# Seven block products for two of the short convolution's three input branches

## The chip, the cores and the metric

The kernel runs on one core of a Trainium2 chip. The metric is the device time of one execution in microseconds (us). A core has a matrix engine (TensorE, PE in the profile; its weight loads are PEld), a vector engine (VectorE, DVE), a scalar engine (ScalarE, ACT), GpSimd (POOL), SyncE (SP), which here only issues transfers, and 16 DMA engines. Matmuls write to PSUM, eight banks of 2 KB on each of 128 partitions; everything else lies in SBUF.

## The reference, cut to what matters

A sequence of 512 tokens of width 1024 passes through a first block (attention with low rank projections, a convolution, a gated feed-forward layer, a gated embedding) and a second block of two layers. The change lies in the second block's first layer:

```python
def short_conv_mixer(h, w_in, conv_w, w_out):
    b_gate, c_gate, u = jnp.split(h @ w_in, 3, axis=-1)      # h: 512 x 1024, w_in: 1024 x 3072
    v = c_gate * u
    vp = jnp.pad(v, ((0, 0), (CONV_WIDTH_2 - 1, 0), (0, 0)))
    conv = sum(conv_w[k] * vp[:, k:k + S] for k in range(CONV_WIDTH_2))
    return (b_gate * conv) @ w_out

h = rms_norm_2(x, norm_mix[0])
x = x + short_conv_mixer(h, a_w_in[0], a_conv_w[0], a_w_out[0])
x = x + squared_relu_mlp(rms_norm_2(x, norm_mlp[0]), mlp_w1[0], mlp_w2[0])
```

Everything is in 32-bit floats.

## The kernel before

Activations lie transposed: a tile holds 128 channels on the partitions and 512 tokens along the free dimension, so 1024 channels are eight tiles, x[0] to x[7]. A 32-bit product is made of three matmuls on rounded parts: each operand is split into a high part (`whi`, `xgh`) and a remainder (`wlo`, `xgl`), and high by high, high by remainder and remainder by high are added in PSUM (L305 to L307 in `mm`).

A weight tile comes from `unit` (L265): SP loads a raw 128 x 1024 tile, ScalarE rounds it to the high part (L280), VectorE subtracts for the remainder (L281). Raw, high and remainder have two buffers each in pool `wp`. `gemm` (L314) multiplies such a tile by the eight tiles of activations: 24 matmuls of 512 columns into one PSUM bank.

The short convolution (L964 to L986) first splits x times the norm's gain into `xg` (L967). Then it runs a loop over eight tiles of output channels c. Each turn makes three gemms: `pc`, `pu` and `pb` (c_gate, u and b_gate). VectorE multiplies pc by the squared row scale R4s (L976) and by pu into the padded tile `gpad` (L979), ScalarE makes the last tap (L981), VectorE adds the other two (L983), multiplies by pb (L985), and the result is split into `hid` (L986). The next loop (L988) makes eight gemms of `hid` with the out weights and adds to x. The PSUM phase in this stage is `ps2` (L859): six banks `mm`, two banks `t`.

The MLP (L995) uses another product, `fast_pair` (L357), for pairs of output tiles. Two output tiles by two halves of the tokens make a 2 x 2 block product, computed with seven block products and not eight. Its moving operands are the two halves of two neighbouring activation tiles (slots B11 to B22) and four sums of them (T1 to T4), formed by `pair_sums` (L323): two scalings on ScalarE into a buffer `yh`, four steps on VectorE into a buffer `yl` (L329 to L332), and a split into `xt`; it is called four times, and `yh` and `yl` have one buffer each. Its weights come from `pair_units` (L339): a raw tile `a` with two weight blocks; a raw tile `s`, loaded by SP and then added to by a second transfer on POOL's queue (L344); a block `z`; two sums of these on VectorE (L351, L353); and the splits of all. `us` and `ua` use the two buffers of `wp`, and `z`, `yh` and `yl` have one each.

Each block product is 12 matmuls of 128 x 256. They run in the order B11, T1, B21, T2, B22, T3, T4. B11, T2, T3 and T4 add up in one bank `y1`, T1 and B22 in a bank `mm`, and each bank is read between two products. `fast_pair` calls `fill` twice between B22 and T4 and twice after T4, and in the MLP a fill is one product of the second layer, 12 matmuls of 512 columns.

The code is written in program order, and a scheduler fixes each engine's own order when the kernel is compiled, earlier places in the program first where instructions are ready; engines run their order in sequence. Buffers are handed out as they come free. SP issues nearly all transfers in one queue. POOL's queue carries `gpad`'s small memset (L978), the additions of L344, and a few elementwise steps.

## Time and profile before

| | us |
|---|---|
| median of 3 runs | 1980.68 |
| lowest, highest | 1980.64, 1984.46 |
| the profiled execution | 1979.01 |
| its span | 1977.2 |
| TensorE busy in it | 1876.5 |
| VectorE busy in it | 1331.9 |
| ScalarE busy in it | 957.0 |

The page of the profile gives busy time by engine, the span in 40 slices, and the chain of work that ended last. The trace can be asked for more: busy time by stretch, instructions in order of time, groups of instructions by line and shape, one line or one tile with what waited for it. A matmul's row gives its start and a modelled duration; as matmuls are pipelined, the distance between two starts is what one costs in a row of them. The short convolution's loop runs from about 713 to 851 us, its out product to 896, the first MLP's paired products from 910 to 1210, the second MLP's from 1632.

### The profile page before, as it was taken

The numbers are of one execution on the slowest core, as the hardware profiler recorded it, in microseconds if no ns is written. First come the engines' busy times: TensorE is split into PE (matmuls) and PEld (weight loads), VectorE is DVE, ScalarE is ACT, GpSimd is POOL, SyncE is SP. The second block draws the span as 40 slices with busy tenths as digits, with TensorE's granted clock in tenths as the row PEclk, the third lists the DMA queues.
The fourth block names the chain that finished last, engine by engine and source line by source line (L and its number), as shares of the span: only waits on it lengthen the run. The fifth ranks groups of instructions, "written<-read, shape, count | busy, mean of one in ns | idle before, by whom it ended". The sixth has DMA issues, their size and how long they took to land.

```text
span 1977.2 us, 27638 instructions
## 1 busy us (share of the span) xinstructions
PE 1876.5 (95%) x10198; PEld 1592.5 (81%) x10198; DVE 1331.9 (67%) x2277; ACT 957.0 (48%) x1755; POOL 420.1 (21%) x397
## 2 busy tenths in 40 slices
PE   8778989999999999999999999989999979999996
PEld 6556788888888978888988988778888778889895
DVE  7979676335444874476666666769887977666664
ACT  6566654333233442254444444546666755444443
POOL 2786240000001420010000002335454420000001
PEclk9889999999999999999999999999999989999998
DMA  4121222223323223233455453254323134554542
GB/s 147 54 67 41 79 82 86 96 96 96 93 90 106 74 76 96 96 119 105 128 144 144 128 141 94 90 163 118 78 84 84 31 100 130 144 132 134 139 107 75
DMA packets 82742, 202.11 MB, mean 102 GB/s; under 512 B 9904, under 2 KB 18288, under 8 KB 82608
## 3 DMA queue, kind: packets, MB, share of 16 engines
q1 hardware_dynamic: 77744, 184.88, 30.7%
q0 software_dynamic: 4032, 14.68, 4.3%
q8 instruction: 80, 1.31, 0.3%
q10 hardware_dynamic: 832, 0.79, 0.1%
q14 instruction: 54, 0.44, 0.1%
HBM read 187.73 MB, written 2.10 MB: 96 GB/s over the span
## 4 chain that ended last, share of the span: by engine, by line
PE 75%; DVE 13%; ACT 4%; issue 3%; DMA 3%; POOL 2%; SPq 0%; DVEq 0%; POOLq 0%; ACTq 0%
PE mm L305 18%; PE mm L306 18%; PE mm L307 18%; PE y L370 3%; PE y L372 3%; PE y L371 3%; DVE cy L605 2%; DVE wlo L281 2%; PE mm L372 2%; PE mm L371 2%; PE mm L370 2%; PE o L530 1%; PE s L497 1%; DVE pw L503 1%; PE t L522 1%
## 5 line engine op out<-in xcount | busy, mean ns | idle before, releaser
L280 ACT CAST whi<-raw 128x512 fp32r<-128x512 f32 (+4 forms) x342 | 260.7, 770 | 469.9 <-PE mm L306 370.7
L281 DVE TENSOR_TENSOR wlo<-raw,whi 128x512 fp32r<-128x512 f32 (+4 forms) x318 | 303.4, 960 | 108.0 <-ACT whi L280 102.6
L306 PE MATMUL mm<-hidl,whi 128*128 128x512 f32 (+1 forms) x794 | 300.1, 379 | 0.1
L305 PE MATMUL mm<-hidh,whi 128*128 128x512 f32 (+1 forms) x794 | 295.1, 379 | 5.1 <-ACT hidh L286 5.0
L307 PE MATMUL mm<-hidh,wlo 128*128 128x512 f32 (+1 forms) x794 | 297.7, 378 | 2.2 <-DVE wlo L281 2.1
L306 PE MATMUL mm<-xgl,whi 128*128 128x512 f32 (+1 forms) x608 | 234.0, 386 | 2.8 <-DVE xgl L290 2.8
L307 PE MATMUL mm<-xgh,wlo 128*128 128x512 f32 (+1 forms) x608 | 233.8, 386 | 0.0
L305 PE MATMUL mm<-xgh,whi 128*128 128x512 f32 (+1 forms) x608 | 232.9, 386 | 0.6 <-ACT whi L280 0.6
L305 PEld LDWEIGHTS mm<-hidh,whi 128*128 128x128 f32 x794 | 148.6, 188 | 32.4 <-ACT hidh L286 5.7
L307 PEld LDWEIGHTS mm<-hidh,wlo 128*128 128x128 f32 x794 | 149.2, 188 | 30.9 <-DVE wlo L281 3.2
L306 PEld LDWEIGHTS mm<-hidl,whi 128*128 128x128 f32 x794 | 149.2, 188 | 27.4 <-DVE hidl L287 0.9
L344 POOL DMA_DIRECT2D raw<-mlp1f x28 | 24.6, 879 | 551.8 <-DVE wlo L281 236.3
L306 PEld LDWEIGHTS mm<-xgl,whi 128*128 128x128 f32 x608 | 115.4, 190 | 28.6 <-DVE xgl L290 4.0
L305 PEld LDWEIGHTS mm<-xgh,whi 128*128 128x128 f32 x608 | 115.2, 190 | 26.0 <-ACT whi L280 1.5
L307 PEld LDWEIGHTS mm<-xgh,wlo 128*128 128x128 f32 x608 | 115.5, 190 | 24.4
L287 DVE TENSOR_TENSOR wlo<-raw,whi 128x1024 fp32r<-128x1024 f32 x56 | 68.5, 1222 | 84.2 <-ACT whi L286 84.1
L421 POOL TENSOR_TENSOR ssq<-ssq,sq 128x512 f32<-128x512 f32 (+1 forms) x58 | 71.4, 1230 | 252.0 <-ACT sq L418 251.1
L505 ACT ACTIVATE pw<-pw,nm 128x512 f32<-128x512 f32 (+3 forms) x160 | 89.4, 560 | 57.7 <-DVE nm L503 55.4
L286 ACT CAST whi<-raw 128x1024 fp32r<-128x1024 f32 x56 | 58.7, 1050 | 97.1 <-DMA raw<-mlp1f 78.4
L1027 DVE TENSOR_TENSOR x<-mm,x 128x512 f32<-128x512 f32 x116 | 79.4, 686 | 37.1 <-PE mm L307 37.0
L603 POOL TENSOR_TENSOR cy<-cy,tap 128x512 f32<-128x512 f32 x60 | 92.0, 1533 | 29.6 <-ACT tap L602 26.0
L605 DVE SCALAR_TENSOR_TENSOR cy<-cp,cols,cy 128x512 f32<-128x512 f32 x60 | 73.3, 1221 | 2.0 <-ACT cy L616 1.4
(835 smaller groups left out, 4695.7 us busy)
## 6 DMA issues: line engine op xcount, KB each, us to landing
raw<-mlp SPq DMA_DIRECT2D x140, 256.0 KB, 2.8
raw<-mlp1f SPq DMA_DIRECT2D x56, 512.0 KB, 3.7
raw<-mlp1f POOLq DMA_DIRECT2D x28, 512.0 KB, 6.5
raw<-a_in SPq DMA_DIRECT2D x24, 512.0 KB, 3.5
raw<-w_gate SPq DMA_DIRECT2D x22, 512.0 KB, 3.5
raw<-w_up SPq DMA_DIRECT2D x22, 512.0 KB, 3.5
raw<-w_down SPq DMA_DIRECT2D x16, 512.0 KB, 3.5
zraw<-mlp1f SPq DMA_DIRECT2D x28, 256.0 KB, 3.7
```

What stands on the lines that cost most here:

```text
L280: S.copy(hi[:, a], raw[:, a])
L281: eng.tensor_tensor(lo[:, a], raw[:, a], hi[:, a], op=OP.subtract)
L305: P.matmul(acc, hi[:, s], h, start=first and k == 0, stop=False)
L306: P.matmul(acc, hi[:, s], l, start=False, stop=False)
L307: P.matmul(acc, lo[:, s], h, start=False, stop=last and k == n - 1)
L370: P.matmul(acc, hi[:, s], h, start=first and j == 0, stop=False, skip_group_check=True)
L371: P.matmul(acc, hi[:, s], l, start=False, stop=False, skip_group_check=True)
L372: P.matmul(acc, lo[:, s], h, start=False, stop=j == 3, skip_group_check=True)
L505: S.activation(t, t, AF.Exp, bias=nm[:, i:i + 1], scale=-1.0, accum_out=rs[:, i:i + 1])
L603: G.tensor_tensor(conv_y[c], conv_y[c], t, op=OP.add)
L605: V.scalar_tensor_tensor(conv_y[c], cp[c][:, k:k + T], w, conv_y[c], op0=OP.mult, op1=OP.add)
L1027: V.tensor_tensor(x[m], acc, x[m], op=OP.add)
```

## The change

For c = 0 the three gemms stay. From c = 1 on, `pc` and `pu` are made by `fast_pair`, with weights packed for `pair_units` on the host (`a_inf`), and `pb` in two halves of 12 matmuls each, whose weights are half units (128 x 512) of a new pool `sw` with two buffers; the two halves are the first two calls of `fill`, and the later calls do nothing. `pair_sums` is called four times when c is 1. `pu` comes out negated, which the step into `gpad` takes back; `pc` and `pu` are now tiles in SBUF. The PSUM phase `ps2m` (two banks `y1`, four `mm`, two `t`) begins ahead of this loop and no longer ahead of the MLP. The pools `sw` and `xta` are released after the loop. The packed tensor `a_in` keeps the tiles that are still read as before.

```diff
--- before.py
+++ after.py
@@ -176,7 +176,9 @@
     A["w_down2"] = _units(w[2048:])
     A["w_ple_proj"] = _units(I["w_ple_proj"][0])
     A["w_ple_gate"] = _units(I["w_ple_gate"][0])
-    A["a_in"] = _units(I["a_w_in_2"][0])
+    w = np.asarray(I["a_w_in_2"][0])
+    A["a_in"] = _units(np.concatenate([w[:, :1152], w[:, 2048:2176]], 1))
+    A["a_inf"] = _blocks(w[:, 1024:].reshape(D, 2, 8, 128).transpose(0, 2, 1, 3)[:, 1:].reshape(D, -1))
     A["a_out"] = _units(I["a_w_out_2"][0])
     for l in range(2):
         A[f"mlp1_{l}"] = _units(I["mlp_w1_2"][l])[:4]
@@ -967,16 +969,32 @@
         split(x[k], *xg[k], col("norm_mix0", k))
     R4 = row_tile(r4)
     R4s = row_tile(r4, square=True)
+    sw, tpl = pool("swa"), pool("xta")
+    psum_phase("ps2m", y1=2, mm=4, t=2)
     hid = []
     for c in range(KT):
-        pc = gemm(A["a_in"][8 + c], xg)
-        pu = gemm(A["a_in"][16 + c], xg)
-        pb = gemm(A["a_in"][c], xg)
-        t = tmp()
+        if c == 0:
+            pc, pu, pb = [gemm(A["a_in"][i], xg) for i in (8, 9, 0)]
+        else:
+            if c == 1:
+                xps = [slots(xg[k:k + 2], pair_sums(k, "norm_mix0", sw, tpl)) for k in range(0, KT, 2)]
+            us = pair_units(A["a_inf"][c - 1], sw)
+            pb = bank("mm")
+            fill = [0, 1]
+
+            def gate_half(i, pb=pb, c=c):
+                u = unit(A["a_in"][c][:, 512 * i:512 * i + 512], pl=sw, size=512, bufs=(2, 2))
+                mm(pb, u, xg[4 * i:4 * i + 4], first=i == 0, last=i == 1)
+
+            pc, pu = fast_pair(us, xps, md, lambda: fill and gate_half(fill.pop(0)))
+        t = tmp() if c == 0 else pc
         V.tensor_tensor(t, pc, R4s, op=OP.mult)
         gpad = md.tile([128, 2 + T], FT, name="gpad", bufs=2)
         G.memset(gpad[:, :2], 0.0)
-        V.tensor_tensor(gpad[:, 2:], pu, t, op=OP.mult)
+        if c == 0:
+            V.tensor_tensor(gpad[:, 2:], pu, t, op=OP.mult)
+        else:
+            V.scalar_tensor_tensor(gpad[:, 2:], pu, -1.0, t, op0=OP.mult, op1=OP.mult)
         y = tmp()
         S.activation(y, gpad[:, 2:], AF.Copy, scale=col("a_conv_w", 3 * c + 2))
         for k in range(2):
@@ -984,6 +1002,8 @@
                                    op0=OP.mult, op1=OP.add)
         V.tensor_tensor(y, pb, y, op=OP.mult)
         hid.append(split_in(md, "hid", y, bufs=9))
+    tpl.release()
+    sw.release()
     sx = SumSq(8, whole=True)
     for m in range(KT):
         acc = gemm(A["a_out"][m], hid)
@@ -1083,7 +1103,6 @@
     def shared_norm(c, ts):
         S.copy(R5[:, ts], rows(c, None, ts)[:, ts])
 
-    psum_phase("ps2m", y1=2, mm=4, t=2)
     mlp(0, md, xg, sx, 5, shared_norm, shared)
     md.release()
     tp[0].release()
```

## Rows read from the trace of the kernel before

**Rows 1.** Part 1 of the page: busy time, share of span, instructions.

```profile
PE 1876.5 (95%) x10198; PEld 1592.5 (81%) x10198; DVE 1331.9 (67%) x2277; ACT 957.0 (48%) x1755; POOL 420.1 (21%) x397
```

**Rows 2.** Part 4 of the page: the chain that ended last, by line.

```profile
PE mm L305 18%; PE mm L306 18%; PE mm L307 18%; PE y L370 3%; PE y L372 3%; PE y L371 3%; DVE cy L605 2%; DVE wlo L281 2%; PE mm L372 2%; PE mm L371 2%; PE mm L370 2%; PE o L530 1%; PE s L497 1%; DVE pw L503 1%; PE t L522 1%
```

**Rows 3.** Busy time by stretch; columns in the first line.

```profile
core 0: us, PE busy (x) PEld busy (x) DVE busy (x) ACT busy (x) POOL busy (x), PEclk, DMA share, GB/s
713.20:726.70 13.50, 13.05 (x52) 10.01 (x52) 8.58 (x15) 5.00 (x8) 1.02 (x1) 0.87 0.10 40
...
735.00:851.00 116.00, 116.00 (x501) 94.05 (x501) 56.47 (x67) 30.81 (x38) 0.60 (x6) 1.00 0.30 97
...
960.00:1200.00 240.00, 240.00 (x1496) 215.38 (x1495) 157.70 (x248) 109.65 (x190) 9.45 (x11) 1.00 0.51 135
1631.80:1652.00 20.20, 17.88 (x105) 15.07 (x105) 17.88 (x30) 12.72 (x23) 0.92 (x1) 1.00 0.56 147
```

**Rows 4.** Timeline, start of the short convolution: start, duration, engine.

```profile
721.53 0.75 DVE L290 SCALAR_TENSOR_TENSOR xgl<-x,cols,xgh 128x512 fp32r<-128x512 f32 x1
...
713.23 0.58 PE L306 MATMUL mm<-xgl,whi 128*128 128x512 f32 x1 [1.81 <-DVE xgl L290]
```

**Rows 5.** Timeline of TensorE, short convolution: first and last of 57 rows.

```profile
759.80 0.39 PE L306 MATMUL mm<-xgl,whi 128*128 128x512 f32 x1
...
772.82 0.39 PE L305 MATMUL mm<-xgh,whi 128*128 128x512 f32 x1
```

**Rows 6.** Timeline of TensorE, first MLP: rows 1 and 49 of 49.

```profile
1005.48 0.28 PE L370 MATMUL y<-xg0h,whi 128*128 128x256 f32 x1
...
1011.18 0.39 PE L305 MATMUL mm<-hidh,whi 128*128 128x512 f32 x1
```

**Rows 7.** View of line 985: durations min/median/max, first and last start.

```profile
L985 DVE TENSOR_TENSOR tmp<-mm,tmp x8: 681/692/692, 740.2 to 851.1; 128x512 f32<-128x512 f32 x8
```

**Rows 8.** View of tile xt0h: one weight load of the MLP.

```profile
L370 PEld LDWEIGHTS mm<-xt0h,whi x28: 187/189/192, 923.3 to 1911.3; 128*128 128x128 f32 x28
```

**Rows 9.** Groups by line and shape, 960 to 1200 us, VectorE: busy, mean ns.

```profile
L281 DVE TENSOR_TENSOR wlo<-raw,whi 128x512 fp32r<-128x512 f32 x46 | 31.0, 684 | 2.5 <-ACT whi L280 2.3
L287 DVE TENSOR_TENSOR wlo<-raw,whi 128x1024 fp32r<-128x1024 f32 x23 | 28.1, 1222 | 37.2 <-ACT whi L286 37.2
...
L287 DVE TENSOR_TENSOR zl<-zraw,zh 128x512 fp32r<-128x512 f32 x11 | 7.6, 692 | 18.0 <-ACT zh L286 18.0
...
L389 DVE TENSOR_TENSOR tmp<-mm,yc 128x256 f32<-128x256 f32 x11 | 4.6, 420 | 6.7 <-PE mm L372 6.7
```

**Rows 10.** Groups by line and shape, 735 to 851 us.

```profile
L983 DVE SCALAR_TENSOR_TENSOR tmp<-gpad,cols,tmp 128x512 f32<-128x512 f32 x16 | 12.0, 749 | 1.1 <-ACT tmp L981 0.8
```

**Rows 11.** Timeline of one pair in the first MLP: ScalarE, VectorE, SP, POOL.

```profile
1008.95 0.37 ACT L397 COPY tmp<-y 128x256 f32<-128x256 f32 x1
...
1010.29 0.69 DVE L351 TENSOR_TENSOR zraw<-raw,zraw 128x512 f32<-128x512 f32 x1
...
1011.00 0.33 SPq L343 DMA_DIRECT2D raw<-mlp1f  x1
...
1013.15 0.68 DVE L287 TENSOR_TENSOR yl<-raw,yh 128x512 fp32r<-128x512 f32 x1
...
1015.20 0.86 POOL L344 DMA_DIRECT2D raw<-mlp1f  x1 [18.00 <-DMA raw<-mlp1f]
```

**Rows 12.** View of line 344, POOL's transfer: time to landing.

```profile
DMA to landing us min/median/max: 5.7/6.5/8.3
```

**Rows 13.** Timeline, start of the second MLP: VectorE, TensorE.

```profile
1623.45 0.42 DVE L329 TENSOR_TENSOR yl<-yh 128x256 f32<-128x256 f32 x1
...
1643.29 1.22 DVE L287 TENSOR_TENSOR xt6l<-yl,xt6h 128x1024 fp32r<-128x1024 f32 x1 [0.52 <-ACT xt6h L286]
...
1636.25 0.38 PE L370 MATMUL mm<-xt0h,whi 128*128 128x256 f32 x1 [1.69 <-DVE tmp L1020]
```

**Rows 14.** Timeline of ScalarE: the last read of the stage before.

```profile
715.96 0.59 ACT L947 ACTIVATE tmp<-mm 128x512 f32<-128x512 f32 x1
```

## Prediction

> **What bounds the kernel now.** I read the page's busy line first. TensorE is busy 1876.5 of 1977.2 us, VectorE 67% of the span [rows 1]; this says only where to look. The chain that ended last is mostly matmul lines, with no vector line above 2% [rows 2]. Then the stage that is changed, in the table of stretches: from 735 to 851 us, TensorE is busy 116.00 of 116.00 us at granted clock 1.00, VectorE 56.47 and ScalarE 30.81 [rows 3]. So the loop over channel tiles is bound by matmuls, and fewer of them shorten it, as long as the rest keeps up. The stretch before (713.2 to 726.7) is another case: TensorE idles and the clock is 0.87, because VectorE hands over the last activations late [rows 3, 4]. The pair of seven products already runs in both MLPs, so nearly every term has a row there.
>
> **The change, part by part.**
>
> *Products.* Neighbouring 512-column matmuls start (772.82 - 759.80)/56 = 0.2325 us apart [rows 5], the 256-column ones of a pair (1011.18 - 1005.48)/48 = 0.1188 us [rows 6]. A channel tile costs three products of 24 matmuls now: 72 x 0.2325 = 16.74 us; seven of them before the last product is read at 851.1 us [rows 7] put the end of the first tile at 733.9. After: 7 x 12 x 0.1188 + 24 x 0.2325 = 9.98 + 5.58 = 15.56 us. Saved: 1.18 us a tile, 8.3 us for seven. This is the whole gain.
>
> A row that could speak against it is the weight load: each takes 189 ns, whatever the columns [rows 8]. It is longer than the 119 ns spacing, yet the spacing in the MLP holds, so loads overlap. The Trainium skill, page "TensorE: Matmul & The Clock Gate", section "Back-to-back issue gap", says that load and product set the spacing together, about 81 ns at 128 columns and 131 ns at 512. By that rule 84 matmuls of 256 columns, at 81 ns or more, would take an estimated 6.8 us or more where 48 of 512 take 6.3, so no gain. The rows disagree with it, 119 against 232 ns, and they decide.
>
> *Vector work of a tile.* Now 56.47/7 = 8.1 us [rows 3]. After, by durations: two 1024-wide remainders 2.44, five 512-wide steps of the pair's weights 3.45, two remainders of the gate's half units 1.37, three sums of halves 1.26 [rows 9]; the conv's own steps t, gpad, two taps, gate, hidl are 0.69 + 5 x 0.7, about 4.3 (the taps by [rows 10]). That is 12.8 us of 15.56, 82%. Neighbouring instructions overlap a little, so perhaps 75%; the MLP has 157.70/240 = 66% with TensorE at 240.00 of 240.00 [rows 3]. VectorE does not become the bound by its sum; by its order it can.
>
> *Order inside a tile.* In the MLP the T4 product's copy starts at 1008.95; the z chunk is freed and added from 1010.29, and the second y remainder starts at 1013.15 and takes 0.68 [rows 11]. T2 and B22 therefore have weights some 4 to 5 us after the last product of the pair before. B11, T1 and B21 cover 36 x 0.1188 = 4.28 us of it. In the MLP two 2.79 us fills stand there too; here the two gate halves are written later, and the conv steps of the tile before (3.7 us on VectorE) have an earlier place in the program. If the scheduled order pulls the gate halves up, the cover is 9.9 us for at most about 8.7; the MLP's order does pull fills forward wherever weights are late. Bounds: nothing, or 8.7 - 4.3 = 4.4 us a tile; I take 0.15 a tile (1 us in all), nearest to the MLP stretch without idle.
>
> *The s chunk.* It is loaded by SP, then added to by a second transfer on POOL's queue. SP issues it at 1011.00, 2.65 us after T4's end (I put that end 0.6 before the copy), and POOL follows at 1015.20 [rows 11], landing 5.7 to 8.3 us later, 6.5 as median [rows 12]. With cast and remainder (1.05 + 1.22) that is 2.65 + 4.2 + 6.5 + 2.6 = 16 us from T4's end to complete weights. They are wanted at T1 of the pair after next, 15.56 + 1.43 = 17.0 us from that same end. In the MLP the period is about 84 x 0.1188 + 48 x 0.2325 = 21.1 us. So the slack falls from some 6.6 to 1 us. SP's queue carries five weight transfers a tile for three: behind a blocked s stand z, a and the gate halves. POOL's has gpad's memset behind the add. I count nothing at 6.5, and 0.8 us a tile at 8.3.
>
> *Start.* Before the first pair four pair sums are formed: each two scalings on ScalarE, four 0.42 us steps, a cast, a 1.22 us remainder. VectorE is full until 721.53 + 0.75 = 722.3 [rows 4]. From there: sums 4 x 2.9 = 11.6, the first pair's weights 5.9, the gate halves 1.4, the first tile's remainder of 1.2 and its conv steps 4.3: 24.4 by duration, about 22.5 with overlap, so 744.8. TensorE's cover until T2 is 733.9 + 0.8 (row tiles) + 4.28 + 5.58 = 744.6. It would just fit, if the sums were not a chain through one pair of buffers. In the second MLP three of them ran from 1623.45 to 1644.5, 7 us each [rows 13]. At 18.5 us (4.6 each: 1.66 + 1.05 + 1.22 + hand-overs) they end at 740.8, at 28 us at 750.3. Bounds: 0 and 7 us, plus a clock loss: after 1.81 us of idle the matmul at 713.23 lasted 0.58 us and not 0.39 [rows 4], while after 1.69 us at 1636.25 the spacing was full again [rows 13]. I take 3 us, as the second MLP's start, which idles 20.2 - 17.88 = 2.3 us [rows 3].
>
> *Banks.* The phase with four mm and two y1 banks begins before this loop, so the first tile waits for banks of the stage before, the last read at 715.96 to 716.6 [rows 14]. TensorE then lacks activations anyway, until 722.3. Bounds 0 to 3 us; I take 0.3. The out product with four banks: a bank is freed under 1 us after its 5.6 us product, three others cover it: 0. *End:* the last product is now T4, with 5 us of conv steps behind it; the first 21 matmuls of the out product do not need the last tile, 4.9 us, and the next unit has as many: 0, at worst 1.
>
> *Sum.* -8.3 + 3 + 1 + 0.3 = -4.0 us. The profiled execution took 1979.01 us (span 1977.2 and 1.8 around it), 1.7 below the median 1980.68. So 1975.0 there, and 1976.7 against the median.
>
> **The rivals.**
> 1. *Start covered.* The sums slip into gaps, the loop has no wait: 1980.68 - 8.3 + 0.5 = 1972.9. For it: from 713.2 to 726.7 VectorE is busy only 8.58 of 13.50 us [rows 3]. Against: the second MLP's start idles, and VectorE is full until 722.3.
> 2. *T2's wait takes the place of the products saved.* Place: between T4 of one tile and T2 of the next, on VectorE's queue. It decides from (8.3 - 3)/7 = 0.75 us a tile on; at 0.9 it gives 1982, at 2.5 a tile -8.3 + 3 + 17.5 = +12, so 1993, slower. For it: cover as written is 4.3 us where the MLP had 9.9. Against: the gate halves are free to move.
> 3. *The added transfer paces the loop.* At 8.3 us of landing 0.8 us a tile: -8.3 + 3 + 5.6 = 1981; it would take 9 us to be clearly slower. The landing is 6.5 at 66% VectorE load; here the load is higher. The Trainium skill, page "SBUF — State Buffer", section "SBUF: two separate sides", says that POOL cannot write descriptors while certain VectorE steps hold the shared port. No row here tells that apart from the read-and-add itself.
> 4. *Loads set the spacing.* 84 x 0.189 + 5.58 = 21.5 us a tile, +33 us: 2013. The MLP rows exclude it nearly; its page stands above.
>
> **How the numbers follow.** Forecast 50% (1974.5 to 1979.5), rival 1 20%, rival 2 17%, rival 3 12%, rival 4 1%. Two parts in a thousand, 4 us, is about what a measurement of this kernel can tell, and the forecast's centre lies on that border. Faster: 26 of the forecast's 50 and all 20: 0.46. Slower: half of rival 2, a third of rival 3, rival 4: 0.13. The rest, 0.41, is same. Range: the low end is the profiled execution with nearly the whole gain, 1979.01 - 8.3 = 1970.7, put at 1971; the high end is rival 2 at 1.1 us a tile with a start of 4 us, 1984.
>
> **What would show it.** Right: 256-column spacing 0.119 us in this stage; a tile's period 15.6 to 15.8 us; idle of about 3 us on TensorE once, between the first tile and the first pair's T1 or T2, ended by a VectorE remainder of xt6 or y; the out product starting some 4 to 5 us earlier than 851. Wrong: periods above 16.5 us with idle ahead of T2 released by a y remainder (rival 2) or ahead of T1 by the s remainder behind its transfer (rival 3); or no idle at all at the start (rival 1). The forecast falls too if later stages move by more than 2 us, since nothing in them is changed.

## The result, and the profile after

The changed kernel takes 2013.21 us (median of 4 runs, 2011.45 to 2015.03); the kernel before, run beside it, 1981.51 us. The ratio is 1.0159, with an interval of 1.0145 to 1.0173: 32 us slower, where 4 us faster was forecast. The profiled execution of the changed kernel took 2011.45 us, its span is 2009.7 us, against 1979.01 and 1977.2.

Part 1 of the page after, which answers to [rows 1]: TensorE is no busier than before in a span that is 32 us longer, so the time is idle time of TensorE.

```profile
PE 1876.3 (93%) x10450; PEld 1603.3 (80%) x10450; DVE 1367.3 (68%) x2360; ACT 989.2 (49%) x1823; POOL 434.7 (22%) x404
```

The table of stretches after, against [rows 3], says where: at the start of the stage (713 to 735 us, 3.85 us busy) and in its loop (735 to 900, 148.19 of 165). The MLP behind it (960 to 1200) has 240 of 240 as before.

```profile
core 0: us, PE busy (x) PEld busy (x) DVE busy (x) ACT busy (x) POOL busy (x), PEclk, DMA share, GB/s
713.00:735.00 22.00, 3.85 (x17) 3.79 (x18) 16.84 (x29) 9.32 (x15) 5.30 (x6) 0.50 0.23 48
735.00:738.00 3.00, 3.00 (x8) 2.32 (x8) 1.86 (x5) 2.24 (x4) 0.00 (x0) 0.50 0.00 0
735.00:900.00 165.00, 148.19 (x882) 129.68 (x882) 97.27 (x146) 63.86 (x106) 5.86 (x12) 0.96 0.41 109
...
960.00:1200.00 240.00, 240.00 (x1486) 214.88 (x1485) 159.32 (x251) 111.35 (x196) 9.54 (x11) 1.00 0.49 132
```

**A length for the stage.** Stages that no edit touches move by some us from kernel to kernel: in the profiles of all kernels below, the stage begins at 687 to 693 us and 1070 to 1082 us follow it. So I measure the stage by itself, in one profiled execution of each kernel: from the first product of `e` with the row scale, in the stage just ahead, to the last addition of the out product. Before:

```profile
689.71 2.74 DVE L948 SCALAR_TENSOR_TENSOR e<-e,cols,R 128x512 f32<-128x512 f32 x4 [0.25 <-ACT R L467]
...
902.99 0.68 DVE L992 TENSOR_TENSOR x<-x,tmp 128x512 f32<-128x512 f32 x1
```

That is 213.3 us. After, in the first two rows of the next fence (timeline of the changed kernel): 250.9 us, 37.6 more; the span grew by 32.5, since the stage began 2.1 us earlier and 3.0 us come back behind it. The rest of the fence is the two places of idle time. All lines of the changed kernel stand two further down than in the kernel before (more from the loop on).

```profile
687.62 4.73 DVE L950 SCALAR_TENSOR_TENSOR e<-e,cols,R 128x512 f32<-128x512 f32 x7 [0.25 <-ACT R L469]
...
938.48 0.69 DVE L1012 TENSOR_TENSOR x<-x,tmp 128x512 f32<-128x512 f32 x1
...
724.36 1.87 PE L438 MATMUL t<-ones,ssq 128*128 128x1 f32 x8 [15.97 <-DVE ssq L423]
733.02 1.94 PE L464 MATMUL t<-ident,r 128*128 128x128 f32 x8 [6.79 <-DVE r L454]
...
734.61 0.78 PE L307 MATMUL mm<-xgh,whi 128*128 128x512 f32 x1
...
798.71 0.28 PE L372 MATMUL y<-xt0h,whi 128*128 128x256 f32 x1
...
800.01 0.28 PE L374 MATMUL y<-xt6h,wlo 128*128 128x256 f32 x1
...
792.37 0.33 SPq L345 DMA_DIRECT2D raw<-a_inf  x1
...
796.40 0.33 SPq L347 DMA_DIRECT2D raw<-a_inf  x1
...
796.50 0.86 POOL L346 DMA_DIRECT2D raw<-a_inf  x1 [18.65 <-ACT whi L282]
...
804.82 1.99 ACT L288 CAST whi<-raw 128x1024 fp32r<-128x1024 f32 x2 [6.69 <-DMA raw<-a_inf]
806.72 0.61 ACT L288 CAST zh<-zraw 128x512 fp32r<-128x512 f32 x1
...
805.92 0.38 PE L372 MATMUL y<-xgh,whi 128*128 128x256 f32 x1 [3.42 <-ACT whi L288]
...
809.38 0.68 DVE L353 TENSOR_TENSOR zraw<-raw,zraw 128x512 f32<-128x512 f32 x1
...
810.13 0.33 SPq L345 DMA_DIRECT2D raw<-a_inf  x1
```

*Start.* TensorE waits 15.97 us for the sum of squares and 6.79 us for the row scale r, with not one product of the first tile between. That product comes at 734.61; before, TensorE was at this stage's products at 713.23 already [rows 4], while the sum of squares was still being made. The products of c = 0 are written into the new PSUM phase, and in TensorE's order everything of the new phase stands behind the last use of the old one, the row scale's matmuls.

*Loop.* One round, read downwards: SP loads s (792.37), the adding transfer is issued when s is there (796.50), the plain chunk a at the same time (796.40), both are awaited until 804.82 by ScalarE, its cast of z stands behind, the sum with z follows (809.38), and only then is the buffer free for the next s (810.13): 17.8 us. TensorE waits meanwhile. Its waits from 735 to 900 us:

```profile
PE y L372 <- ACT whi L288: 8.9, 4, 3.4
PE mm L372 <- ACT whi L288: 2.3, 3, 1.4
PE mm L307 <- ACT hidh L288: 1.8, 1, 1.8
```

The first line is B11 in four rounds, which needs the weights of chunk a; the second is T1, which needs chunk s. So the chunk that TensorE waits for here is mostly a, which lands together with the added s. Where the add's cost is taken apart below, this changes from kernel to kernel.

The time to landing of the adding transfer (view of line 346) and of the plain chunk a (line 347) in the same stretch; the first answers to [rows 12]:

```profile
DMA to landing us min/median/max: 6.2/8.2/8.4
...
DMA to landing us min/median/max: 3.4/7.5/8.3
```

The eight multiplications by the gate (line 985 before, [rows 7]) now lie from 753.2 to 892.0:

```profile
L1003 DVE TENSOR_TENSOR tmp<-mm,tmp x8: 679/684/691, 753.2 to 892.0; 128x512 f32<-128x512 f32 x8
```

### The profile page after: what moved, and what is told of

It reads as the page before. It is cut to its first block, busy times and chain, and to the rows that moved or that the text cites. A ratio compares the mean times of both kernels' runs of the same rounds, so it can differ in the third digit from the quotient of the medians.

```text
span 2009.7 us, 28386 instructions
## 1 busy us (share of the span) xinstructions
PE 1876.3 (93%) x10450; PEld 1603.3 (80%) x10450; DVE 1367.3 (68%) x2360; ACT 989.2 (49%) x1823; POOL 434.7 (22%) x404
## 5 line engine op out<-in xcount | busy, mean ns | idle before, releaser
L282 ACT CAST whi<-raw 128x512 fp32r<-128x512 f32 (+5 forms) x335 | 247.2, 746 | 402.1 <-PE mm L308 317.5
L283 DVE TENSOR_TENSOR wlo<-raw,whi 128x512 fp32r<-128x512 f32 (+3 forms) x311 | 285.9, 926 | 110.8 <-ACT whi L282 107.4
L308 PE MATMUL mm<-xgl,whi 128*128 128x512 f32 (+1 forms) x496 | 190.5, 385 | 1.8 <-DVE xgl L289 1.1
L309 PE MATMUL mm<-xgh,wlo 128*128 128x512 f32 (+1 forms) x496 | 189.7, 383 | 0.0
L307 PE MATMUL mm<-xgh,whi 128*128 128x512 f32 (+1 forms) x496 | 189.6, 385 | 0.0
L289 DVE TENSOR_TENSOR wlo<-raw,whi 128x1024 fp32r<-128x1024 f32 x70 | 85.5, 1223 | 112.3 <-ACT whi L288 112.1
L288 ACT CAST whi<-raw 128x1024 fp32r<-128x1024 f32 x70 | 73.1, 1049 | 138.4 <-DMA raw<-mlp1f 87.6
L308 PEld LDWEIGHTS mm<-xgl,whi 128*128 128x128 f32 x496 | 94.6, 191 | 21.9 <-DVE xgl L289 1.9
L309 PEld LDWEIGHTS mm<-xgh,wlo 128*128 128x128 f32 x496 | 94.7, 191 | 19.5
L307 PEld LDWEIGHTS mm<-xgh,whi 128*128 128x128 f32 x496 | 94.4, 191 | 19.1
```

The costliest lines, as they stand in the source:

```text
L282: S.copy(hi[:, a], raw[:, a])
L283: eng.tensor_tensor(lo[:, a], raw[:, a], hi[:, a], op=OP.subtract)
L288: S.copy(h, src)
L289: (eng or V).tensor_tensor(l, src, h, op=OP.subtract)
L307: P.matmul(acc, hi[:, s], h, start=first and k == 0, stop=False)
L308: P.matmul(acc, hi[:, s], l, start=False, stop=False)
```

## The experiments

The table holds each kernel's ratio to the kernel before, run on the same chip at the same time; the length of the stage as defined above; and the mean distance of the gate multiplications from the second to the seventh (from the third where two tiles are plain), so in tiles that are made by pairs; 16.73 is the old spacing.

| kernel | ratio, interval | stage, us | distance, us |
|---|---|---|---|
| before | 1 | 213.3 | 16.73 |
| after | 1.0159 (1.0145 to 1.0173) | 250.9 | 19.94 |
| e1_phase_late | 1.0153 (1.0124 to 1.0183) | 245.0 | 18.90 |
| e2_phase_early | 1.0049 (1.0027 to 1.0072) | 224.4 | 16.73 |
| e3_no_add | 1.0076 (1.0047 to 1.0105) | 228.2 | 15.90 |
| e4_late_no_add | 1.0078 (1.0058 to 1.0098) | 226.3 | 16.00 |
| e5_no_phase | 1.0130 (1.0101 to 1.0160) | 235.5 | 17.87 |
| e6_no_phase_no_add | 0.9984 (0.9969 to 1.0000) | 218.5 | 16.08 |
| e7_pool_sum | 1.0030 (1.0010 to 1.0050) | 221.8 | 15.81 |
| e8_a_buffer | 1.0014 (0.9992 to 1.0036) | 225.6 | 17.19 |
| e9_sums_late | 1.0031 (1.0018 to 1.0044) | 218.8 | 15.91 |
| e10_pool_sum_late | 1.0030 (1.0019 to 1.0041) | 223.4 | 16.07 |
| e11_copy_on_vector | 1.0128 (1.0109 to 1.0146) | 239.4 | 19.09 |
| e12_gate_last | 1.0028 (1.0015 to 1.0040) | 220.1 | 15.63 |
| e13_two_plain | 1.0040 (1.0027 to 1.0052) | 217.3 | 15.80 |
| e14_two_plain_gate_last | 1.0038 (1.0025 to 1.0052) | 217.9 | 15.79 |
| e15_gate_held | 1.0017 (1.0004 to 1.0031) | 215.5 | 15.39 |
| e16_two_plain_gate_held | 1.0001 (0.9987 to 1.0014) | 214.3 | 15.97 |
| e17_z_ahead | 1.0077 (1.0058 to 1.0095) | 228.5 | 16.62 |

e7 and e12 have the same order of TensorE's matmuls in this stage and differ by 1.7 us in it, so I take a difference of 2 us in that column for none. e7, e8, e10 and e12 to e17 have, for room, two square buffers in this stage in place of three; no kernel tries that alone.

### The PSUM phase

**The phase change alone, in the kernel before.**

```diff
+    psum_phase("ps2m", y1=2, mm=4, t=2)
     hid = []
...
-    psum_phase("ps2m", y1=2, mm=4, t=2)
     mlp(0, md, xg, sx, 5, shared_norm, shared)
```

> The kernel before, with nothing changed but the place of the PSUM phase change, which now stands ahead of the short convolution's loop. Theory P: TensorE idles some 20 us from 710 us on and the time is about 2000 us, though no pair exists in this stage. Rival V, or banks alone (four in place of six): within 3 us of the kernel before, 1981.

Measured: 1992.51 us, 10 us slower, the stage 11.1 us longer with no pair in it. TensorE's waits (705 to 900 us) are those of the changed kernel, shorter by the pair sums that VectorE does not have here:

```profile
PE t L436 <- DVE ssq L421: 11.2, 1, 11.2
PE t L462 <- DVE r L452: 2.2, 1, 2.2
```

So the drain (TensorE standing empty until the old banks have had their last use) is the phase's own doing, if smaller than expected: 13.4 us of waits, and not some 20. The loop behind it runs at the old 16.73.

**The phase change one tile later.**

```diff
-    psum_phase("ps2m", y1=2, mm=4, t=2)
     hid = []
...
             if c == 1:
+                psum_phase("ps2m", y1=2, mm=4, t=2)
```

> The changed kernel, with the change of PSUM phase moved from ahead of the loop to the turn c = 1. Theory P (the early phase change puts the first tile's 72 matmuls behind the row scale's matmuls in TensorE's order, which idles 16.0 and 6.8 us there): the two waits vanish, about 20 us come back, 1992 us, the first tile's matmuls start near 711 us. Rival V (VectorE's pair sums, slipped in ahead of x and xgl, hold the first tile up): still about 2012 us, with the first tile's matmuls waiting for xgl.

Measured: 2012.14 us, no gain that can be told, though the stage is 5.9 us shorter. The drain has moved, from the row scale's matmuls to the last reader of the old banks, the first tile's gate multiplication (TensorE's waits, 705 to 900 us):

```profile
PE y L372 <- DVE tmp L1003: 7.7, 1, 7.7
PE mm L309 <- DVE wlo L283: 5.1, 2, 4.7
```

**No phase change inside the stage.** The pairs use the `mm` banks of the old phase for y1, and the change stands ahead of the MLP again.

```diff
-        y1 = bank("y1")[:, :H]
+        y1 = bank("y1" if "y1" in banks else "mm")[:, :H]
...
-    psum_phase("ps2m", y1=2, mm=4, t=2)
     hid = []
...
+    psum_phase("ps2m", y1=2, mm=4, t=2)
     mlp(0, md, xg, sx, 5, shared_norm, shared)
```

> The changed kernel without any PSUM phase change in this stage: the pairs take their y1 bank from the six mm banks of ps2, and the change to ps2m stands ahead of the MLP as in the kernel before. Theory B (a phase change drains TensorE: nothing of the new phase starts before the last read of the old one, 22.8 us of idle in the changed kernel, 13.4 with the phase alone, 7.7 plus 4.7 with the phase at c = 1): no wait over 3 us from 705 to 760 us, about 1992 to 1995 us, the loop's idle of 16 us unchanged. Rival V (VectorE's extra sums ahead of xgl and the row scale are the cause by themselves): still 10 us of idle or more in that stretch, 2005 us.

Measured: 2009.55 us. The stage is 15.4 us shorter than after and the drain is gone (the longest wait left from 705 to 760 us is 3.2), but the total is only about 6 us shorter, where about 20 were expected: later stages take 1082 us here against 1071 after. Why those are slower I did not find out.

In this kernel the loop waits for the other chunk: T1, for s, 6.1 us in all, B11 and B21, for a, 1.7. Chunk a lands in 4.4 us here, as median (view of line 347), and not in 7.5:

```profile
793.59 0.40 PE L372 MATMUL mm<-xt0h,whi 128*128 128x256 f32 x1 [2.15 <-ACT whi L288]
...
DMA to landing us min/median/max: 3.6/4.4/6.6
```

### The adding transfer

**No adding transfer.**

```diff
-        nc.gpsimd.dma_start(s, src[:, 2048:3072], accum_op=OP.add)
+        if add:
+            nc.gpsimd.dma_start(s, src[:, 2048:3072], accum_op=OP.add)
```

> The changed kernel without POOL's adding transfer for the seven pairs of the convolution, so that their s chunk holds a wrong weight block. Theory D (in the loop the plain transfer of chunk a starts together with the adding one and lands after 7.5 us in place of 4, and ScalarE's casts that wait for it hold up the z cast and the T4 copy behind them): a lands in about 4 us, the loop's 16 us of TensorE idle shrink to under 4, about 1999 us, the start unchanged. Rival Q (VectorE's order, conv steps ahead of the y remainders): the loop's idle stays, about 2011 us.

Measured: 1996.84 us, the stage 22.7 us shorter than after and the tiles 15.90 apart, against the forecast's 15.6 to 15.8. The plain chunks land in 4.0 us (median, transfers of 735 to 900 us), and from 735 us on the longest wait is 1.6 us, at the out product's start. The start changed too, which was not expected: of the 22.7 us, 4.3 lie ahead of the first gate multiplication. In the changed kernel VectorE stood 3.63 us at its sum with z until the first adding transfer landed, and the steps of the row scale r stood behind that sum; TensorE waited 6.79 us for r there and waits 2.6 here (VectorE after, then two lines of e3):

```profile
728.61 0.69 DVE L353 TENSOR_TENSOR zraw<-raw,zraw 128x512 f32<-128x512 f32 x1 [3.63 <-DMA raw<-a_inf]
...
PE t L465 <- DVE r L455: 2.6, 1, 2.6
...
raw<-a_inf SPq DMA_DIRECT2D x13, 512.0 KB, 4.0
```

**No adding transfer, and the phase change one tile later.**

```diff
-            us = pair_units(A["a_inf"][c - 1], sw)
+                psum_phase("ps2m", y1=2, mm=4, t=2)
+            us = pair_units(A["a_inf"][c - 1], sw, add=False)
```

> Both edits: the phase change at c = 1, and no adding transfer for the convolution's pairs (wrong weights in their s chunk). If P and D are the two causes and add up: about 1978 us, 3 us under the kernel before, with the loop near 15.6 us a tile. If the first pair's chain of sums now costs what was forecast, 3 us of idle ahead of its T1 or T2. Under rival Q about 1990 us.

Measured: 1996.25 us, as e3 and not the 1978 expected; TensorE waits 8.6 us once for the first tile's gate multiplication.

**Neither phase change nor adding transfer** (the edits of e5 and e3).

```diff
-    psum_phase("ps2m", y1=2, mm=4, t=2)
...
+            us = pair_units(A["a_inf"][c - 1], sw, add=False)
```

> As the run without a phase change, and without POOL's adding transfer in the convolution's pairs (wrong weights in their s chunk). If both causes are removed: the forecast's own terms are left, 8.3 us of products saved less some 3 to 5 us at the start, so 1977 to 1980 us. If 1985 or more, a third cause is open, most likely VectorE's sums ahead of xgl.

Measured: 1981.64 us, ratio 0.9984. The four kernels after, e3, e5 and e6 are a table of two causes: the phase costs the stage 9.7 us without the add (e3 less e6) and 15.4 with it, the add 17.0 without the phase and 22.7 with it. Of the 17.0, 3.5 lie ahead of the first gate multiplication, 12.6 between the first and the last, and 0.9 behind. Yet the stage of e6 is still 5.2 us longer than before, not 4 shorter. Its timeline shows where:

```profile
692.99 1.41 DVE L951 SCALAR_TENSOR_TENSOR e<-e,cols,R 128x512 f32<-128x512 f32 x2 [0.25 <-ACT R L470]
...
741.82 0.36 PE L373 MATMUL mm<-xgh,whi 128*128 128x256 f32 x1
...
850.93 0.40 PE L307 MATMUL mm<-hidh,whi 128*128 128x512 f32 x1
...
911.45 0.68 DVE L1012 TENSOR_TENSOR x<-x,tmp 128x512 f32<-128x512 f32 x1
```

The first pair product comes 48.8 us into the stage; the second tile began 733.9 - 689.7 = 44.2 us into it before: 4.6 us lost at the start. The first matmul of the out product comes 157.9 us into it, 3.3 earlier than before, but 24 pair products (2.9 us) follow it, so the loop gave 5 us of its 8.3. And the out product ends 8.4 us later after its first matmul than before: these 2.9 us, and 5.5 for the last tile's chain, while TensorE idles and then runs at a lower clock (stretches of e6):

```profile
864.00:868.00 4.00, 1.92 (x6) 0.97 (x6) 3.13 (x7) 2.61 (x5) 0.00 (x0) 1.00 0.37 131
868.00:872.00 4.00, 2.50 (x7) 1.45 (x8) 4.00 (x6) 3.34 (x6) 0.00 (x0) 0.93 0.22 74
872.00:876.00 4.00, 4.00 (x13) 3.12 (x12) 4.00 (x6) 1.42 (x3) 1.52 (x1) 0.65 0.69 252
```

### What in the loop hangs on the transfer

**T4's copy on VectorE** (on e5).

```diff
-        S.copy(t2[:, :H], y1)
+        (t4 or S.copy)(t2[:, :H], y1)
...
+            pc, pu = fast_pair(..., t4=V.tensor_copy)
```

> As e5_no_phase (no bank change inside the stage, adding transfer kept), with the copy of T4's bank in the convolution's pairs on VectorE instead of ScalarE. In e5 seven T4 copies lay 18.0 us apart on average, and the copy stood behind ScalarE's casts of the next tile's chunks, which waited for their transfers. Theory A (the blocked queue of ScalarE carries the delay from the transfers to TensorE and to the release of the buffers): spacing 16 to 17 us, time 8 to 15 us below e5 (2009.6). Theory B (the late chunks themselves are what TensorE lacks, and who copies does not matter): spacing 17.5 to 18.5, time within 4 us of e5.

Measured: 2008.87 us, as e5, and tiles 19.09 apart, more than either theory said. The copy that stood behind ScalarE's casts is not what delays TensorE: theory A falls. The longest wait is still for the casts themselves (735 to 900 us):

```profile
PE mm L372 <- ACT whi L288: 9.5, 6, 3.7
```

**z's cast ahead of the others** (on e5; two buffers for the converted z).

```diff
+        uz = z_first and split(z, *(pl.tile([128, 512], FR, name=f"z{p}", bufs=2) for p in "hl"))
         ua, us = [split(r, *(wp.tile([128, 1024], FR, name=w, bufs=2) for w in ("whi", "wlo"))) for r in (a, s)]
...
-    temp_phase("tp4", tmp=4, ssq=2, sq=3)
+    temp_phase("tp4", tmp=4, ssq=2, sq=2)
```

> As e5_no_phase (no bank change inside the stage, adding transfer kept), with two buffers for the converted z chunk, so that ScalarE converts it while the T4 product of the tile before still reads the other one, ahead of the s chunk's cast instead of behind both casts. Complete computation. In the changed kernel one round was: s issued by SP at 792.37, the adding transfer issued at 796.50 and landed at about 804.7, both casts from 804.82, z's cast at 806.72 behind them, the sum with z at 809.38, the next s issued at 810.13, so 17.8 us. Theory C (these steps are one closed loop, and z's cast behind the blocked casts is a link of it): the loop is shorter by the 1.9 us or so of z's cast and remainder, T4 tiles 1 to 2 us closer on average than e5's 17.9 us, the stage 7 to 14 us shorter than e5's 235.5. Theory D (the landings alone set the distance): spacing within 0.5 us of 17.9 and the stage within 3 us of e5's.

Measured: 1999.03 us, 10 us below e5; the stage is 7.0 us shorter, the low end of theory C. But the distances are 17.1, 18.7, 18.0, 17.5 and then 11.8, so the mean of 16.62 rests on the last. And the adding transfers land sooner here too, 5.9 us as median against 6.9 in e5: how much of the gain is z's cast as a link of the loop and how much the landing is not told apart.

```profile
raw<-a_inf POOLq DMA_DIRECT2D x6, 512.0 KB, 5.9
```

**A buffer of its own for a** (no phase change; the add is kept).

```diff
-        a, s = [wp.tile([128, 1024], FT, name="raw", bufs=2) for _ in range(2)]
+        a = pl.tile([128, 1024], FT, name="araw") if own else wp.tile([128, 1024], FT, name="raw", bufs=2)
+        s = wp.tile([128, 1024], FT, name="raw", bufs=2)
```

> As the run without a phase change, adding transfer kept, but chunk a has a raw buffer of its own and chunk s has the two of wp (and two square buffers for room). Theory D1 (the s chain paces the loop: its add lands late): s can be loaded a turn ahead, the loop's idle goes, 1980 us. Theory D2 (chunk a, which is loaded only after its last reader and lands late beside the add, paces it): little changes, 1990 us or more.

Measured: 1986.42 us with runs from 1977.09 to 1993.38, so not told from the kernel before; the profiled execution is the slowest of the eight. In it the stage is 9.9 us shorter than e5's, the tiles 17.19 apart.

The step of theory D1 is there: s is issued a turn ahead, the second pair's at 736.18 us (746.22 in e5), the last pair's at 815.07 (839.37). TensorE's wait for s (T1) falls from 6.1 us to 0.4. But its wait for a (B11 and B21) rises from 1.7 to 6.0, so the loop's idle time does not go. Chunk a is still loaded only after its last reader, still beside the add, and lands no sooner than in e5: 4.6 us as median for 4.4, and 7.60 and 8.05 in two rounds. So what was gained is the s chain, and a, which theory D2 named, then paces the loop. Of the 9.9 us, 5.1 lie ahead of the last gate multiplication and 4.8 in the out product behind it; why those, is not shown.

```profile
736.18 0.33 SPq L346 DMA_DIRECT2D raw<-a_inf  x1
...
810.86 0.39 PE L373 MATMUL mm<-xgh,whi 128*128 128x256 f32 x1 [2.66 <-ACT whi L288]
...
araw<-a_inf SPq DMA_DIRECT2D x6, 512.0 KB, 4.6
```

**s summed by GpSimd from two plain transfers** (no phase change).

```diff
-        nc.gpsimd.dma_start(s, src[:, 2048:3072], accum_op=OP.add)
+            s2 = pl.tile([128, 1024], FT, name="s2")
+            nc.sync.dma_start(s2, src[:, 2048:3072])
+            G.tensor_tensor(s, s, s2, op=OP.add)
```

> As the run without a phase change, with the sum of the s chunk made by GpSimd from two plain transfers in the convolution (and two square buffers in place of three in this stage, for room). Theory D (the adding transfer and what collides with it pace the loop): as without the add, within 4 us of that run, about 1980 us. If GpSimd's 2 us a sum hold up VectorE or the sum lands as late as the adding transfer did: 1988 or more.

Measured: 1989.65 us, ratio 1.0030; tiles 15.81 apart, as without any sum. So in the loop neither the sum nor the loading of a second block costs anything; the adding transfer does. That transfer differs in three ways: it adds in the tile that the first one wrote, it goes out only when the first has landed, and POOL issues it. Which of the three costs the time is not told apart. The time itself is on the side of 1988 or more, and its interval lies above e6's. Of the stage's 3.3 us over e6, all lie ahead of the first gate multiplication (60.3 us into the stage, 56.9 in e6); whether they come from the sum, the extra load or the square buffer given up is not shown.

### What is left: start and end of the stage

**The pair sums behind the last split**, on e6 and on e7.

```diff
+                with tc.issue_after(xgh_end.ins), tc.issue_after(xgl_end.ins):
-                xps = [slots(xg[k:k + 2], pair_sums(k, "norm_mix0", sw, tpl)) for k in range(0, KT, 2)]
+                    xps = [slots(xg[k:k + 2], pair_sums(k, "norm_mix0", sw, tpl)) for k in range(0, KT, 2)]
```

> As e6_no_phase_no_add (no bank change inside the stage, the adding transfer left out, so the s blocks are unsummed and the output of the branches is not the reference's), and besides the four pair sums are queued on VectorE and ScalarE behind the last split of the inputs instead of between the gated updates. In e6 the last low part was written about 10 us later than before the change and TensorE had 21.7 of 27 us busy between 713 and 740. Theory (the sums stand ahead of the row's last splits on the in-order engines and the first tile pays for it): TensorE 25 us or more of those 27, the first T4 copy some 4 us earlier, time 4 to 6 us below e6, 1976 to 1978 beside a kernel before at about 1982. Rival (the sums are needed as soon as tile 1 begins, so the wait only moves from the splits to xt6): the same time as e6 within 2 us, with TensorE waiting on xt4 or xt6 about 740.

> As e7_pool_sum (no bank change inside the stage, s summed by GpSimd from two plain transfers), with the pair sums queued behind the last split. Complete computation. Theory (what was left of e7's loss was the start): 4 to 6 us below e7, which was 5 us above the kernel before on its chip, so within 2 us of the kernel before. Rival (VectorE or GpSimd in the loop holds e7 back, not the start): no nearer than 4 us above the kernel before.

Measured: 1989.37 and 1988.49 us, stages 218.8 and 223.4, no better than e6 and e7: both theories fall. In e9 TensorE is busy 21.15 of the 27 us, not 25. With the splits first it waits elsewhere instead, in e10 2.6 us for xt6. The rivals are not shown either: e9's time is above e6's, interval and all, though its stage is not (later stages take 1076 us for 1070), and it has no wait for xt4 or xt6; e10 is 5 us above the kernel before, as its rival said, but nothing here shows that the loop holds it.

**Two plain tiles** (six by pairs), on e10.

```diff
-        if c == 0:
-            pc, pu, pb = [gemm(A["a_in"][i], xg) for i in (8, 9, 0)]
+        if c < 2:
+            pc, pu, pb = [gemm(A["a_in"][i], xg) for i in (8 + c, 10 + c, c)]
```

> As e10_pool_sum_late (pair sums behind the last split, s summed by GpSimd, no bank change), with the first two tiles instead of one computed by three full products; six tiles by pairs, so one tile's saving of 1.2 us is given up. Complete computation. In e10 TensorE was busy 38.1 of 47 us between 713 and 760, in the kernel before 46.1. Theory (the loss at the start is that the pair sums and the first pair's chunks are not ready behind one tile of cover): TensorE 43 us or more of those 47, out product's last addition 4 to 7 us earlier than e10's 914.9, time 3 to 6 us below e10. Rival (the loss at the start is VectorE's load ahead of the splits or the granted clock, which a second plain tile does not change): within 2 us of e10.

Measured: TensorE is busy 42.62 of 47 us at the start, e10 38.13 (713 to 760 us, e13 and then e10), and the stage is 6.1 us shorter.

```profile
713.00:760.00 47.00, 42.62 (x183) 33.92 (x184) 41.16 (x62) 25.28 (x35) 6.46 (x8) 0.89 0.26 84
```

```profile
713.00:760.00 47.00, 38.13 (x183) 31.01 (x183) 38.84 (x57) 23.55 (x35) 8.78 (x8) 0.89 0.30 96
```

But the median is 1990.76 us, ratio 1.0040, no lower than e10's. The profiled execution was the shortest of ten (1985.01); that the start is covered shows in it alone, and a gain in the time was not shown.

**The last tile's gate products at the end**, first by their place in the program (on e7), then held on TensorE's queue behind T4.

```diff
-            fill = [0, 1]
+            fill = [None, None, 0, 1] if c == KT - 1 else [0, 1]
```

> As e7_pool_sum (no bank change inside the stage, s summed by GpSimd), with both halves of the last tile's gate product behind its T4 product instead of between the block products. Complete computation. In e7 the last gate multiplication came at 865.6 us, 18.7 after the one before, TensorE then waited 2.1 us for the last tile's high part and the last addition of the out product came at 914.2, 11.3 us later than before the change. Theory (the last tile's convolution chain lies open behind T4, where in the kernel before 24 gate products of 5.6 us cover it): no wait of TensorE for the last high part over 0.5 us, the out product's last addition 3 to 5 us earlier relative to the first gate multiplication, time 2 to 5 us below e7. Rival (the out product's first banks already cover the chain and the loss lies elsewhere): the out product ends where e7's does, within 1 us.

Measured: 1987.33 us, and no test of the theory, for the scheduler left the gate products where they were; TensorE's order in the stage is e7's.

```diff
+                    with tc.issue_after(t4_last[0].ins):
+                        mm(pb, u, xg[4 * i:4 * i + 4], first=i == 0, last=i == 1)
```

> As e12_gate_last, with the last tile's 24 gate products held on TensorE's queue behind the last T4 product; in e12 they still stood ahead of it, in the order of e7, so that e12 did not try the theory. Complete computation. In e12 the last pair product went out at 854.7 and the last tile's high part came at 861.65 after a wait of 1.8 us; 860 to 868 had 5.2 of 8 us busy at 0.84 and 0.73 of the clock, in the kernel before 8 of 8 at 1.00. Theory (the chain behind T4 lies open there because no gate products cover it): 24 products of 5.6 us run behind T4, TensorE's waits for the last high and low part fall under 0.5 us in sum, the clock stays at 1.00, and from the first gate multiplication to the last addition of the out product 155 to 157 us instead of 158.6 in e12. Rival (TensorE only does the same work in another order, what is moved behind T4 is missing before it): within 1 us of e12's 158.6.

Measured: 1985.29 us. The stretch 860 to 868 us of e12 and then of e15:

```profile
860.00:868.00 8.00, 5.19 (x13) 2.99 (x14) 7.04 (x12) 5.79 (x10) 0.00 (x0) 0.79 0.29 98
```

```profile
860.00:868.00 8.00, 8.00 (x36) 6.41 (x35) 5.14 (x8) 4.49 (x6) 0.00 (x0) 1.00 0.42 141
```

The waits for the last hid parts are gone, the clock stays at 1.00, and the stage is 4.6 us shorter than e12's. From the first gate multiplication to the end it is 157.4 us against 158.6, short of the 155 to 157 expected. But that mark has moved: it comes 58.1 us into the stage here and 61.5 in e12. The seventh comes at 154.3 and 154.7, and from there to the end it is 61.2 us against 65.4. So some 4 us were gained at the end. The medians differ by 0.1%, within their intervals.

**Both**, first with e12's edit, then with e15's.

```diff
+        if c < 2:
...
+            fill = [None, None, 0, 1] if c == KT - 1 else [0, 1]
...
+                    with tc.issue_after(t4_last[0].ins):
```

> As e13_two_plain and e12_gate_last together, complete computation. If both theories hold (start covered by a second plain tile, end by the last gate product): out product's last addition 8 to 11 us earlier than e10's 914.9, 904 to 907, and the time within 0.2% of the kernel before or up to 4 us below it. If only one of them holds, 3 to 6 us above e14's best case; if neither, as e10, 5 us above the kernel before.

> As e14_two_plain_gate_last with the last tile's gate products held behind the last T4 product. Complete computation. e14's out product ended at 906.7, 3.7 us later than in the kernel before. If the end's theory holds, 902 to 904, and the time within 0.2% of the kernel before or below it; if not, as e14, 0.4% above.

Measured: 1989.49 us for e14, whose order on TensorE is e13's and which is as e13; 1981.96 us for e16, ratio 1.0001, the stage 214.3 us, 1.0 more than before. Its last addition comes at 907.4 us, not at 902 to 904, as its stage begins 4.4 us later than e14's; the stage is 3.6 us shorter. With no phase change, no adding transfer, two plain tiles and a covered end, pairs in this stage are worth nothing that can be measured. No version was faster than the kernel before beyond its interval; e6, which leaves out a sum that must be made somewhere, touches 1.0000.

## Why the prediction was wrong

Taken by its steps, in us of the stage; the sum of what was measured is -8.3 + 9.7 + 17.0 + 5.7 (phase and add together, beyond each alone; it lies in the loop, and where it comes from is not shown) + 13.5 (start, loop and end, from e6) = 37.6.

- *Products, -8.3: right.* The 256-column spacing is (800.01 - 798.71)/11 = 0.118 us in this stage too, and the tiles lie 15.4 to 16.1 us apart wherever the adding transfer is out (15.56 forecast). The weight load of 189 ns does not set the spacing, so rival 4 is out, and that its 2013 us is the measured time is chance. The Trainium skill, page "TensorE: Matmul & The Clock Gate", section "Back-to-back issue gap", gives about 131 ns at 512 columns; the rows have 232 [rows 5]. Nothing hung on it.
- *Vector work: right.* VectorE is busy 97.27 of 165 us from 735 to 900, and in e3, where the loop has its forecast length, 58.78 of 79.5 us from 776.8 to 856.3: 74%, where 75% was forecast. It is not the bound by its sum. By its order it can hold others up, as at the start, where the row scale stood behind the sum with z.
- *Order inside a tile, 1: right in kind, and rival 2 is out.* TensorE's waits ahead of T2 and B22 (for yh or yl) are 0.8 us in sum at most, in any kernel. But the loop of e6 still gives 3.3 us less than its products saved, and not 1 less.
- *Banks, 0.3 with bounds 0 to 3: wrong*, the first failing step. It asked when the old banks would be read out (716 us, [rows 14]) and not where the new phase puts everything in TensorE's order. Its last old users are the matmuls of the row scale, which end a chain over VectorE, at 733 us. Before, the first tile's 16.7 us of products hid that chain. e2 shows 11.1 us in the stage with nothing else changed; here 9.7 to 15.4, as the pair sums and the first pair's weights stand in VectorE's order too (e2's wait of 11.2 becomes 16.0, and 16.1 in e3).
- *The s chunk, "I count nothing", and rival 3, 1981: wrong in size*, the second failing step. The chain that it laid out was the right one. By its own steps, from T4's end (789.8): issue 2.6, until POOL's issue 4.1 (2.65 and 4.2 forecast), landing 8.2 (6.5), and two casts with their remainders, since a lands beside s, 3.5 (2.6 for one): 18.4, where the forecast wanted s after 17.0. And the lateness feeds back: z's cast stands behind the blocked casts, so in the next round SP issues s 7.6 us after T4's end (802.49 to 810.13) and not 2.65. The forecast took the worst landing and one late tile after another at 0.8 us; the loop is closed, and the add cost 17 us (e6 to e5), 12.6 of it between the first and the last gate multiplication.

  Chunk a, which lands beside the add and is loaded only after its last reader, was not costed at all; in the changed kernel B11 and B21 wait 10.4 us for it and T1 2.3 for s, in e5 1.7 and 6.1, in e8 6.0 and 0.4. So the two are late together, and which of them TensorE waits for depends on the kernel. With z's cast ahead of them (e17) 10 us come back, but the adding transfers land sooner there too, so that this step is the one that closes the loop is likely and not shown by itself.

  The Trainium skill, page "SBUF — State Buffer", section "SBUF: two separate sides", says that POOL cannot write its descriptors while certain VectorE steps hold the shared port. No run here tests it; the longer landings came at a lower load of VectorE, 59% of 735 to 900 us against 66% in the MLP [rows 3].
- *Start, 3 with bounds 0 to 7: right in size, not in place.* It is 4.6 in e6. Forecast was a wait behind the first tile, for xt6 or y; in e6 TensorE waits within the first tile, 4.3 us for the last splits (xgl; 1.8 before), which the sums delay. Only with the splits first does it wait for xt6 (e10).
- *End, 0, at worst 1: wrong*, by some 5, the third failing step. The first 21 matmuls of the out product were to cover the conv steps behind T4; in e6 TensorE waits 3.6 us between 864 and 872 and then works at 0.65 to 0.93 of its clock. In the kernel before the gate's 5.6 us of products stood between. With them there again the wait is gone and some 4 us come back (e15).

The forecast said that the out product would start 4 to 5 us before 851; even in e6 its first matmul comes 3.3 us earlier in the stage, and 24 pair products are still to follow. Rival 3 had the mechanism and 12%; no rival had the phase change or the end, and the slower side was given 13% in all.

## What to carry to other kernels

A change of PSUM phase is a barrier in TensorE's order: before moving one, look for the last matmul that uses the old banks, what chain it waits for, and which products hid that chain until now. A pipeline that was copied from another loop should be checked as a closed loop of its buffers (load, second load, casts, sum, release) against the shorter period of the new one; slack of 1 us in 17 is none when two transfers land side by side. And at the end of a loop, ask which independent work stands between the last product and the chain behind it. When two loads land together, removing the wait for one can bring out the wait for the other.

## What the runs showed of the hardware

An adding transfer of 512 KB landed in 5.9 to 8.2 us (medians of e17 and after). A plain one of the same size (chunk a) issued less than 1.1 us from it took 7.5 to 8.3 us in the last four rounds of the changed kernel, but 3.6 to 6.6 in five rounds of e5; what makes that difference is not shown. Chunk s, issued some 4 us ahead of its add, took 3.4 to 3.9 in both.

After the idle time at the start, TensorE's granted clock was 0.50 (1.2 GHz) from 735 to 738 us, with 512-column matmuls 0.43 us apart, and full again from 740. A much shorter gap did the same: in e7, after some 2.5 us of idle at the end of the stage, it was at 0.50 (1.2 GHz) for eight us (stretches of e7).

```profile
864.00:868.00 4.00, 1.56 (x6) 0.65 (x4) 3.06 (x5) 2.42 (x4) 0.00 (x0) 0.96 0.24 81
868.00:872.00 4.00, 3.90 (x8) 2.17 (x8) 3.12 (x6) 3.08 (x4) 0.00 (x0) 0.50 0.35 127
872.00:876.00 4.00, 3.55 (x9) 2.67 (x9) 4.00 (x5) 3.14 (x6) 1.52 (x1) 0.50 0.48 157
876.00:880.00 4.00, 4.00 (x15) 3.21 (x14) 2.16 (x6) 1.05 (x1) 0.00 (x0) 0.76 0.28 105
```

By these rows, as an estimate, the lower clock cost 3.90 x 0.50 + 3.55 x 0.50 + 4.00 x 0.24 = 4.7 us, more than the idle before it.
